# Where the rows of the transposed x begin inside a tile, in the feed-forward blocks of an encoder layer

## The chip, the cores and the metric

The kernel runs on one core of one Trainium2 chip. The metric is the device time of one execution in microseconds (us), given as the median of several runs. Beside the runs there is one profiled execution, whose trace lists every instruction with its start and its duration; it has its own time, which differs a little from the median.

Engine names are those of the profile: PE is the matrix engine (TensorE), PEld is the part of it that loads the stationary operand of a matmul, DVE is VectorE, ACT is ScalarE, POOL is GpSimd, SP issues most of the DMAs.

## The reference

One encoder layer on x of 512 rows by 1024 columns, all in float32. It has three residual blocks, each between two RMS norms:

```python
h = swiglu(rmsnorm(x, norm_ffn1_pre), w_ffn1_in, w_ffn1_out)      # feed-forward 1
x = x + 0.5 * rmsnorm(h, norm_ffn1_post)
h = mixer(rmsnorm(x, norm_mix_pre), w_mix_in, ..., w_mix_out)      # conv and mLSTM
x = x + rmsnorm(h, norm_mix_post)
h = swiglu(rmsnorm(x, norm_ffn2_pre), w_ffn2_in, w_ffn2_out)      # feed-forward 2
x = x + 0.5 * rmsnorm(h, norm_ffn2_post)

def swiglu(x, w_in, w_out):                # w_in 1024 x 5632, w_out 2816 x 1024
    gate, up = split(x @ w_in, 2)
    return (silu(gate) * up) @ w_out
```

The change touches the operand x of `x @ w_in` in the two feed-forward blocks. The mixer takes its x from tiles that another branch of the same function makes, and these stay as they are.

## The kernel before, in words

**Numbers in two parts.** A float32 number is held as a high part (rounded to the matrix engine's fp32r) and a low part (what is left), made by `split`: ACT writes the high part, DVE subtracts. A product is the sum of three matmuls: high by high, high by low, low by high.

**Feed-forward, first half.** The hidden width 2816 is 22 column blocks of 128. Each has a gate block and an up block of `w_in`. The first two (`PLAIN = 2`) are computed plainly by `plain` (L545): for one half of the 512 rows of x, 24 matmuls (3 parts by 8 chunks of the contraction) of 256 columns. The other 20 take gate and up together in a scheme with seven products instead of eight: `w_pair` makes sums and differences of the weight blocks on DVE and splits them, and `mm_part` (L519) runs each product as 12 matmuls (3 parts by 4 chunks) of 256 columns. So one column block is 84 matmuls at L519, one block of the network 20 times 84 = 1680 of them and 8 times 24 = 192 at L545; both feed-forward blocks together have 3744.

**Operands of these matmuls.** The weights are stationary: 128 columns of a `whi`, `wlo` or `ws` tile, loaded anew for each matmul. The transposed x is the moving operand: 256 columns. It lies in eight tiles per block, made by `xq_tile` and cut by `xq_hl`: four for the quarters of x (half of the width by half of the rows) and four, `t1` to `t4`, for the combinations that the seven products need (`combine_x`). Each tile has four rows `q`, one for each chunk of the contraction. In a row the first 256 numbers are the high part and the next 256 the low part. A matmul reads 256 numbers of one row, 1024 bytes in each partition, and consecutive matmuls of a product go through the rows q = 0, 1, 2, 3.

**Where the rows lie.** All tiles of the pool `big` are made by `wide` with 4 times 528 = 2112 numbers, 8448 bytes, in each partition (L64). In the built program the pool's first tile starts at byte 24256 of a partition, and the others follow every 8448 bytes. 8448 is 33 times 256, so all tiles start 192 bytes behind a multiple of 256. Most users take the first 2048 numbers as four rows of 512 (`bigt`, L67): rows 2048 bytes apart, which all start at the same place within 256 bytes. The x tiles of the feed-forward are cut by L407 into four rows of 528 instead: 2112 bytes apart, so that each starts 64 bytes further within 256 than the one before. The weight tiles all start 192 bytes behind a multiple of 256, and so do their blocks of 128 numbers (512 bytes).

**Other matmuls that matter here.** In the mixer, `seven` calls the same `mm_part` with x tiles of the `"m"` branch, made by `bigt`: there all rows start at the same place. L726 is the second half of the feed-forward (`product_out`), with 512 columns of weights as the moving operand; its operands too start at that one place. L953 is the mixer's v projection: x is stationary there, and the moving operand is a weight tile of four rows of 528 (`v_split`), in pairs of matmuls of 256 and of 272 columns.

**What sets the order.** A scheduler places the instructions of each engine; `pin` holds some of them in the order of the program. Weights are fetched by SP through `w_load` and split one block ahead by `w_split`.

Of the kernel before, what the change touches and what calls it, by code (L numbers as in the profile page):

```python
# [8 lines left out]
F32 = mybir.dt.float32  # L9
F32R = mybir.dt.float32r  # L10
# [26 lines left out]
BW = 528  # L37
# [4 lines left out]
def encoder_kernel(ctx: ExitStack, tc: tile.TileContext, a: dict, out: bass.AP):  # L42
# [16 lines left out]
    def nm(s):  # L59
        uid[0] += 1  # L60
        return f"{s}_{uid[0]}"

    def wide(dt=F32):
        return big.tile([P, 4 * BW], dt, tag="big", name=nm("big"))  # L64

    def bigt(dt=F32):
        return wide(dt)[:, 0:2048].rearrange("p (q f) -> p q f", q=4)  # L67

    def ps():
        return psum.tile([P, 512], F32, tag="ps", name=nm("ps"))  # L70
# [333 lines left out]

    def xq_tile(xq, key):
        if key not in xq["q"]:
            xq["q"][key] = bigt(F32R) if "m" in xq else wide(F32R).rearrange("p (q f) -> p q f", q=4)  # L407
        return xq["q"][key]

    def xq_hl(xq, key):  # L410
        if "m" in xq and isinstance(key, tuple):
            return tuple(xq_tile(xq, (key[0], v))[:, :, blk(key[1], 256)] for v in "hl")
        t = xq_tile(xq, key)
        return t[:, :, 0:256], t[:, :, 256:512]

    def flip_q(tb, xs, xq, halves=(0, 1), bank=None):

        full = []
        for b in halves:
            pt = bank or ps()  # L420
            for k in range(4):
                pin(nc.tensor.transpose(out=pt[:, blk(k)], in_=xs[:, blk(4 * b + k)], identity=ident))  # L422
            hi, lo = xq_hl(xq, (b, tb // 2))
            split(hi[:, :, blk(tb % 2)], lo[:, :, blk(tb % 2)], ch(pt))
            if b not in xq["f"]:
                xq["f"][b] = bigt()
            if bank:
                return lambda fn: pin(fn(xq["f"][b][:, :, blk(tb)], ch(pt)))
            full.append((b, pt))
        for b, pt in full:  # L430
            pin(nc.scalar.copy(xq["f"][b][:, :, blk(tb)], ch(pt)))
# [74 lines left out]
    def mm_cols(o, w, xq):  # L506
        n = 0
        for ww, xx in ((0, "h"), (0, "l"), (1, "h")):
            for k in range(KD):
                nc.tensor.matmul(  # L510
                    o, w[ww][:, k, :], xq_tile(xq, (k // 4, xx))[:, k % 4, FULL], start=n == 0, stop=n == 3 * KD - 1)
                n += 1
# [10 lines left out]
    def ffn(xq, between, finish, mid=None, within=None, ahead=(2, 2, 1, 1), late=None, prep=None, block=0):  # L523
# [4 lines left out]


        h = [bigt() for _ in range((NF + 3) // 4)]  # L530
        spare.extend(h[-1][:, q, 0:512] for q in (2, 3))

# [399 lines left out]
    xq = st["xq"]  # L932
# [2 lines left out]
        return xq_hl(xq, (k // 4, tb // 2))[hl][:, k % 4, blk(tb % 2)]  # L935


    vaug = wide().rearrange("p (q f) -> p q f", q=4)
    vv = vaug.rearrange("p c (h e) -> p c h e", e=BW // 4)
    nc.gpsimd.memset(vv[:, :, :, DV:DV + 1], 1.0)  # L940
    spread = t2()
# [308 lines left out]
        pn2[:, 256:272], parl, acd.rearrange("p q c -> p (q c)"),  # L1250
        start=True, stop=True,
    )
    Ct = wide().rearrange("p (q f) -> p q f", q=4)
    Cf = Ct.rearrange("p q f -> p (q f)")
    Cs = Cf[:, 0:12 * 129].rearrange("p (q i e) -> p q i e", q=4, i=3)
    nat1 = Cf[:, 1552:2064].rearrange("p (c r) -> p c r", r=P)
# [215 lines left out]
```

## Time and profile before

| what | value |
|---|---|
| median of 3 runs | 885.02 us (884.16 to 885.32) |
| the profiled execution's own time | 884.01 us |
| its span in the trace | 882.1 us |
| mean granted TensorE clock | 0.998 |
| PE busy | 873.4 us, 99% of the span |
| DVE busy | 731.5 us, 83% |
| ACT busy | 492.9 us, 56% |

The span runs from the first instruction to the last of the profiled execution; 1.9 us of its time lie around it. Durations in the groups are those of single instructions. Matmuls overlap each other, so the duration of one (280 ns in the feed-forward) is more than the distance from one start to the next; that distance is had from the chain of waits, which lists stretches of the chain with their length and their count of instructions.

### The profile page before, as it was taken

The page shows a single profiled execution, that of the slowest core. Times are in us where ns is not written, and L with a number is a line of the kernel's source. Part 1 is how long each engine was busy: PE and PEld are TensorE (multiplying, and loading weights), DVE is VectorE, ACT ScalarE, POOL GpSimd, SP SyncE. Part 2 cuts the span into 40 slices and gives each one's busy share as a digit, 9 for nine tenths or more (in the row PEclk, how much of TensorE's full clock was granted, in tenths as well). Part 3 has the DMA queues.
Part 4 walks back from the last instruction along what each step waited for, and adds up shares of the span by engine and source line. Part 5 has one row for each costly group of instructions (what it writes and reads, how often), then busy time and mean ns, then how long its engine had stood idle before and what let it go on. Part 6 is the DMA issues. An engine that isn't in the chain of part 4 may idle for free.

```text
span 882.1 us, 15403 instructions
## 1 busy us (share of the span) xinstructions
PE 873.4 (99%) x6039; PEld 808.1 (92%) x6039; DVE 731.5 (83%) x1159; ACT 492.9 (56%) x855; POOL 93.6 (11%) x123
## 2 busy tenths in 40 slices
PE   8999999999999999999999999999999999999997
PEld 7999999999988889988998988999999999988885
DVE  7989898988889978887588757897898888869956
ACT  7655556544657645755475536555555555546722
POOL 5000000001232023100121011000000000223000
PEclk9999999999999999999999999999999999999999
DMA  9444333435998852442063733433333423899722
GB/s 263 121 121 134 106 95 98 120 88 130 227 246 200 279 180 86 121 119 72 1 191 96 223 112 106 130 100 97 96 96 98 138 77 109 202 243 229 268 74 95
DMA packets 140384, 123.24 MB, mean 140 GB/s; under 512 B 5500, under 2 KB 116112, under 8 KB 140312
## 3 DMA queue, kind: packets, MB, share of 16 engines
q1 hardware_dynamic: 129936, 97.62, 37.0%
q0 software_dynamic: 10368, 24.65, 12.6%
q8 instruction: 47, 0.77, 0.4%
q14 instruction: 25, 0.20, 0.1%
q10 hardware_dynamic: 8, 0.01, 0.0%
HBM read 115.96 MB, written 6.29 MB: 139 GB/s over the span
## 4 chain that ended last, share of the span: by engine, by line
PE 98%; DVE 0%; ACT 0%; issue 0%; POOL 0%; DVEq 0%; POOLq 0%; ACTq 0%
PE ps L519 48%; PE ps L726 19%; PE ps L510 9%; PE ps L545 5%; PE ps L1428 5%; PE ps L748 5%; PE ps L953 3%; PE ps L1331 1%; PE ps L422 1%; PE ps L1339 0%; PE ps L475 0%; PE ps L1280 0%; PE ps L1307 0%; PE ps L1300 0%; PE ps L1373 0%
## 5 line engine op out<-in xcount | busy, mean ns | idle before, releaser
L519 PE MATMUL ps<-big,whi 128*128 128x256 f32 x2064 | 284.1, 281 | 0.0
L519 PEld LDWEIGHTS ps<-big,whi 128*128 128x128 f32 x2064 | 261.4, 188 | 1.1 <-ACT t L1312 0.2
L366 ACT CAST whi<-raw 128x1024 fp32r<-128x1024 f32 x170 | 175.6, 1051 | 68.5 <-DVE raw L219 23.7
L369 DVE TENSOR_TENSOR wlo<-raw,whi 128x1024 fp32r<-128x1024 f32 x166 | 201.1, 1218 | 12.1 <-ACT whi L366 7.8
L519 PE MATMUL ps<-big,wlo 128*128 128x256 f32 x1032 | 161.8, 280 | 0.0
L519 PEld LDWEIGHTS ps<-big,wlo 128*128 128x128 f32 x1032 | 139.0, 189 | 0.0
L726 PE MATMUL ps<-whi,big 128*128 128x512 f32 x336 | 105.7, 389 | 0.0
L726 PEld LDWEIGHTS ps<-whi,big 128*128 128x128 f32 x336 | 62.9, 188 | 13.0
L519 PE MATMUL ps<-big,ws 128*128 128x256 f32 x516 | 70.0, 280 | 0.0
L173 POOL DMA_DIRECT2D raw<-in_w_ffn_out_dram x18 | 22.2, 1232 | 442.3 <-DMA raw<-in_w_ffn_out_dram 226.3
L519 PEld LDWEIGHTS ps<-big,ws 128*128 128x128 f32 x516 | 64.8, 188 | 0.0
L726 PE MATMUL ps<-wlo,big 128*128 128x512 f32 x168 | 64.8, 389 | 0.0
L693 ACT COPY t<-ps 128x256 f32<-128x256 f32 x40 | 14.9, 373 | 88.4 <-PE ps L519 88.4
L510 PE MATMUL ps<-big,whi 128*128 128x512 f32 x224 | 54.5, 394 | 0.0
L366 ACT CAST whi<-t 128x1024 fp32r<-128x1024 f32 (+1 forms) x44 | 39.5, 914 | 17.7 <-DVE t L219 10.2
L510 PEld LDWEIGHTS ps<-big,whi 128*128 128x128 f32 x224 | 41.4, 188 | 8.7
L369 DVE TENSOR_TENSOR wlo<-t,whi 128x1024 fp32r<-128x1024 f32 (+1 forms) x44 | 46.1, 1048 | 1.4 <-ACT whi L366 0.7
L748 PE MATMUL ps<-whi,big 128*128 128x512 f32 x128 | 39.8, 390 | 0.0
L726 PEld LDWEIGHTS ps<-wlo,big 128*128 128x128 f32 x168 | 31.5, 188 | 6.5
L695 DVE TENSOR_TENSOR t<-ps,t 128x256 f32<-128x256 f32 x40 | 16.9, 422 | 21.0 <-PE ps L519 20.9
L545 PE MATMUL ps<-big,whi 128*128 128x256 f32 x256 | 33.6, 282 | 0.0
L698 ACT ACTIVATE t<-t 128x512 f32<-128x512 f32 x40 | 25.2, 631 | 12.4 <-DVE t L695 12.0
(245 smaller groups left out, 1412.3 us busy)
## 6 DMA issues: line engine op xcount, KB each, us to landing
raw<-in_w_ffn_in_dram SPq DMA_DIRECT2D x68, 512.0 KB, 4.8
raw<-in_w_ffn_out_dram SPq DMA_DIRECT2D x26, 512.0 KB, 4.2
raw<-in_w_mix_in_dram SPq DMA_DIRECT2D x24, 512.0 KB, 4.2
t<-in_w_ffn_in_dram SPq DMA_DIRECT2D x20, 512.0 KB, 3.8
raw<-in_w_ffn_out_dram SPq DMA_DIRECT2D x36, 256.0 KB, 5.0
raw<-in_w_ffn_out_dram POOLq DMA_DIRECT2D x18, 512.0 KB, 7.8
xd<-x POOLq DMA_DIRECT2D x8, 512.0 KB, 2.9
x<-xd POOLq DMA_DIRECT2D x8, 512.0 KB, 5.2
```

Of the source, the lines that this page charges most:

```text
L173: nc.gpsimd.dma_start(sums.rearrange("p (g f) -> p g f", g=2), top[:, 512:1024].rearrange("p (g f) -> p g f", g=1).broadcast_to([P, 2, 512 ...
L366: latest["hi"] = nc.scalar.copy(out=hi, in_=src)
L369: latest["lo"] = eng.tensor_tensor(out=lo, in0=src, in1=f32(hi), op=ALU.subtract)
L510: nc.tensor.matmul(o, w[ww][:, k, :], xq_tile(xq, (k // 4, xx))[:, k % 4, FULL], start=n == 0, stop=n == 3 * KD - 1)
L519: pin(nc.tensor.matmul(o, ww[:, k, :], x[xx][:, k, :], start=first and n == 0, stop=n == 11, skip_group_check=True))
L545: pin(nc.tensor.matmul(o, ww[:, k, :], xq_hl(xq, (k // 4, th))[xx][:, k % 4, :], start=n == 0, stop=n == 3 * KD - 1))
L695: nc.vector.tensor_tensor(out=c[:, h1], in0=y[:, h0], in1=a_[:, h1], op=ALU.add)
L698: mark["act"] = nc.scalar.activation(c, c, AF.Silu)
L726: nc.tensor.matmul(acc[tb + t][half], left[n][x][:, blk(t)], right[n][y], start=first and x == y == 0, stop=last_ and x == 1, skip_group_c ...
L748: nc.tensor.matmul(acc[tb][half], hT[hh][:, blk(tb)], w[ww][:, blk(half, 512)], start=fresh and hh == ww == 0, stop=k == NF - 1 and hh == ...
L953: nc.tensor.matmul(pv_[i][:, 0:at.stop - at.start], xv(xx, k, tb), ww[:, k % 2, at], start=n == 0, stop=n == 3 * KD - 1)
L1428: nc.tensor.matmul(acc[half], yy[yi][:, k % 4, blk(tb)], wmo[k][wi][:, blk(half, 512)], start=(n == 0 and yi == 0 and wi == 0), stop=(n == ...
```

## The change

The x tiles of the feed-forward get rows of 512 numbers, 2048 bytes apart, and the first row begins 48 numbers (192 bytes) behind the tile's start. 48 + 4 times 512 is 2096 of the tile's 2112 numbers. All four rows of all eight tiles then start 192 + 192 = 384 bytes behind a multiple of 256, which is 128 bytes behind the next one. The tiles themselves, their number and their places stay. The two other edits write `wide` with a rearrangement as `bigt(row=BW)`, which is the same tile with the same rows.

The instructions of all five engines, their order and the semaphores that they wait for are the same in both built programs; the programs differ in the addresses with which the x tiles are written and read.

```diff
-    def bigt(dt=F32):
-        return wide(dt)[:, 0:2048].rearrange("p (q f) -> p q f", q=4)
+    def bigt(dt=F32, at=0, row=512):
+        return wide(dt)[:, at:at + 4 * row].rearrange("p (q f) -> p q f", q=4)
...
     def xq_tile(xq, key):
         if key not in xq["q"]:
-            xq["q"][key] = bigt(F32R) if "m" in xq else wide(F32R).rearrange("p (q f) -> p q f", q=4)
+            xq["q"][key] = bigt(F32R) if "m" in xq else bigt(F32R, at=48)
         return xq["q"][key]
...
-    vaug = wide().rearrange("p (q f) -> p q f", q=4)
+    vaug = bigt(row=BW)
...
-    Ct = wide().rearrange("p (q f) -> p q f", q=4)
+    Ct = bigt(row=BW)
```

## The prediction

> **What bounds the kernel now.** I read the page first, for what the end hangs on.
>
> ```profile
> span 882.1 us, 15403 instructions
> PE 98%; DVE 0%; ACT 0%; issue 0%; POOL 0%; DVEq 0%; POOLq 0%; ACTq 0%
> PE ps L519 48%; PE ps L726 19%; PE ps L510 9%; PE ps L545 5%; PE ps L1428 5%; PE ps L748 5%; PE ps L953 3%; PE ps L1331 1%; PE ps L422 1%; PE ps L1339 0%; PE ps L475 0%; PE ps L1280 0%; PE ps L1307 0%; PE ps L1300 0%; PE ps L1373 0%
> ```
>
> The chain that ended last is the matrix engine for 98% of the span, and L519 alone, the products of the feed-forward's first half, is 48% of it. So what counts is the distance from one matmul to the next. It is not in the groups, whose durations overlap, but in the chain of waits, where a piece has a start, a length and a count. These pieces have no gap in them:
>
> ```profile
> 22.68 13.25 PE ps L545 x112
> 35.93 196.41 PE ps L519 x1668
> 236.51 83.00 PE ps L726 x366
> 343.07 8.76 PE ps L953 x72
> ...
> 560.79 11.28 PE ps L545 x96
> 572.07 193.44 PE ps L519 x1644
> ```
>
> And a piece of the same L519 in the mixer, from the chain of a window there:
>
> ```profile
> 484.99 8.64 PE ps L519 x72
> ```
>
> Length by count gives the step. In the feed-forward it is 196.41 / 1668 = 117.75 ns and 193.44 / 1644 = 117.66 ns, so 117.7. In the mixer the same helper, with the same shapes, steps by 8.64 / 72 = 120.0 ns. What differs there is how the x tile is cut: the mixer's rows all start at one place within 256 bytes (192 bytes behind a multiple), the feed-forward's start at 192, 0, 64 and 128 in turn. So the placement of the moving operand has a price, and the trace shows two of its values.
>
> The groups of weight loads in windows of the two stages (first 40 to 220 us, then 485 to 493.6 us) say where it sits:
>
> ```profile
> L519 PEld LDWEIGHTS ps<-big,whi 128*128 128x128 f32 x878 | 110.7, 188 | 0.0
> ...
> L519 PEld LDWEIGHTS ps<-big,whi 128*128 128x128 f32 x39 | 5.0, 192 | 0.0
> ```
>
> The load of the next weights, which runs beside the matmul, takes 188 ns on average in the feed-forward and 192 ns in the mixer. Load and matmul seem to get in each other's way when both read at the same place within 256 bytes (the weights always start at 192), and the next matmul starts later.
>
> **The fixed part of a step.** L726 moves 512 columns and has both operands at the place 192: 83.00 / 366 = 226.8 ns. Against the mixer's 120.0 ns for 256 columns, 256 more columns cost 106.8 ns. So a step is 106.8 ns for each 256 columns and a fixed part:
>
> - both operands at 192, 256 columns: 120.0 - 106.8 = 13.2 ns; by this split the same for 512 columns;
> - the feed-forward, rows in turn at 192, 0, 64, 128: 117.7 - 106.8 = 10.9 ns;
> - L953, pairs of 256 and 272 columns, 264 on average: 8.76 us / 72 = 121.7 ns, less 106.8 * 264 / 256 = 110.1, leaves 11.5 or 11.6; I use 11.5. Its moving rows are also 2112 bytes apart, but in other shares: of 12 matmuls four read at 192, four at 0, two at 64, two at 128.
>
> **The change part by part.**
>
> *The refactored lines* (`vaug`, `Ct`) are the same tiles with the same rows: nothing. No instruction, wait, semaphore or DMA is added, removed or moved; no queue is passed.
>
> *The writes into the x tiles* are 128 numbers per row in `flip_q` and 256 in `combine_x`, on ACT and DVE. Their count and shape stay; I cost them at nothing, and bound that: DVE has room, as the window of the first block shows, so that a slowdown of some of these few writes would be covered.
>
> ```profile
> 36.00:232.00 196.00, 196.00 (x1667) 196.00 (x1666) 172.50 (x273) 103.43 (x169) 5.01 (x4) 1.00 0.42 117
> ```
>
> The columns are the window, its length, then PE, PEld, DVE, ACT, POOL busy. DVE works 172.5 of 196 us. The matmuls here could become 10% faster before DVE's work alone filled the stage, so DVE doesn't eat a gain of one or two per cent.
>
> *The reads* are the whole term. 2 blocks times (20 times 84 + 8 times 24) = 3744 matmuls read the moved rows, and all are in pieces like those above, on the path. One ns of the step is 3.74 us of the whole. After the change all their rows start at 128, with the weights still at 192. No stage of this trace has that all the time, so the fixed part at 128 has to be bounded.
>
> First reading: each place has its own price, and the feed-forward's 10.9 is their mean. Then 0, 64 and 128 together have 4 * 10.9 - 13.2 = 30.4, 10.1 each: a step of 116.9, 0.8 ns less, 3.0 us.
>
> Second reading, with L953 for a second equation: 12 * 11.5 = 138 = 4 * 13.2 + 4 p(0) + 2 (p(64) + p(128)). With the sum 30.4 this gives p(0) = 12.2, and 9.1 for each of 64 and 128: a step of 115.9, 1.8 ns less, 6.7 us.
>
> Between these two I take 1.07 ns, 4.0 us, nearer the first, since in the second an error of 0.1 ns in 11.5 moves p(128) by 0.3.
>
> Bounds beyond: the durations of single matmuls in the first block (least, median, greatest) are
>
> ```profile
> L519 PE MATMUL ps<-big,ws x240: 276/280/284, 37.2 to 225.0; 128*128 128x256 f32 x120
> L519 PE MATMUL ps<-big,ws x12: 283/283/283, 486.3 to 487.6; 128*128 128x256 f32 x12
> ```
>
> 280 goes with a step of 117.7 and the mixer's 283 (second row) with 120.0. If every one took the least, 276, the step would be about 4 ns less, 15 us in all: 870 us. That is the far end below. Above, nothing in the trace is worse for 256 columns at a fixed place than the mixer's 120.0: 2.3 ns more, 2.3 * 3.744 = 8.6 us. A gain can't be excluded by a row, a loss neither.
>
> Sum: 884.0 - 4.0 = 880.0 us for an execution like the profiled one (span 882.1 and 1.9 around it). The median of the runs shown is 1.0 us above the profiled time, so I forecast 885.0 - 4.0 = 881.0 us.
>
> [...]
>
> **The rivals.**
>
> *The price is for repeating, not for the place.* What the mixer has in common with the changed kernel is that each row starts at the same place as the row before. If stepping on by 64 bytes from matmul to matmul is what breaks up a regular meeting of load and matmul, the changed kernel falls into the mixer's rhythm: 120.0 ns, 885.0 + 8.6 = 893.6 us, slower by 1%. For it: the mixer's duration is 283/283/283 in the row above, a locked rhythm, while the feed-forward spreads from 276 to 284; and L726, with everything at one place, has the same 13.2. Against it: both rows that show the 13.2 have the matmul and the load at the *same* place, and the change makes it 128 beside 192; and L953, where each place comes at least twice running, has 11.5 and not 13.2. It decides from a fixed part above 10.9 at place 128.
>
> *Nothing happens.* [...] The mixer's 120.0 could come from something else in that stage (its neighbours on the engine, other traffic), and the placement be indifferent: 885.0 us. For it: only 72 matmuls in one piece carry the 120.0. Against it: weight loads at L519 are the same shape in both stages and DVE, ACT and DMA are no busier there, as the window of that piece shows (DVE 6.84 of 8.6 us, 80%; the first block above has 88%):
>
> ```profile
> 485.00:493.60 8.60, 8.60 (x74) 8.60 (x74) 6.84 (x15) 6.56 (x16) 1.32 (x1) 1.00 0.40 125
> ```
>
> *A place with no meeting at all.* If 64 bytes behind the load is far enough that the two never collide, the step goes to the 276 ns rows: about 870 us. For it: single durations of 276 occur. Against it: a fixed part of 10.9 - 4 = 6.9 ns is below both readings above.
>
> *The change doesn't do what it says.* All x reads come from `xq_hl`, so the new rows reach every one of the 3744; I give this no chance of its own.
>
> **How the numbers follow.** The forecast (gain of 2 to 7 us, a fixed part of 9 to 10.4) has 0.48; a gain beyond that, towards 870, 0.10; nothing, within 0.2% (1.8 us, about what a measurement of this kernel can tell from no change), 0.14; the repeat price, in full or in part, 0.28. So faster 0.58, same 0.14, slower 0.28. The likeliest case's own range is 878 to 883. For 8 in 10 it must reach to the repeat price, 893.6, and down to the second reading's 6.7 us with a little more: 877.5. What is left out is most of the 0.10 below.
>
> **What would show it right or wrong.** In the changed kernel's chain the long L519 pieces should be about 1650 matmuls in 116.6 ns each, 193 us in place of 196.4 (count alike); the weight loads of L519 in 40 to 220 us should have a mean of 187 or 188 with no tail to 193; the mixer's 120.0 and L726's 226.8 should stay. If the repeat price rules, L519 shows 120.0 ns and loads of 192 in the feed-forward too. If nothing happens, 117.7 stays. I am wrong in the working if the total moves and the L519 step doesn't: then the path would run through DVE or ACT in these stages, and the waits of PE there would no longer be empty.

## The result, and the profile after

| | before | changed |
|---|---|---|
| median | 885.17 us (884.16 to 886.24, 4 executions) | 869.81 us (868.84 to 870.57, 4 executions) |
| ratio to before | | 0.9825, 95% interval 0.9813 to 0.9837 |
| the profiled execution | 884.01 us, span 882.1 | 868.84 us, span 867.0 |

The kernel became faster by 1.75%, 15.4 us, where I had forecast 4 us. The time lies outside my range, at the far end that I had priced as a rival. These four executions lie at 869 to 871 us; other executions of the same program, below, took up to 878. Two executions of kernels tried below, of 1661.35 and 887.31 us, count as slow and enter no median and no ratio.

The pieces of the chain of waits of the changed kernel (start, length, what, count) that answer to those of before:

```profile
22.97 12.87 PE ps L545 x112
35.84 189.04 PE ps L519 x1668
229.03 82.96 PE ps L726 x366
...
477.46 8.64 PE ps L519 x72
...
553.22 10.88 PE ps L545 x96
564.10 186.32 PE ps L519 x1644
```

The two long L519 pieces have the counts of before and are 7.37 and 7.12 us shorter: 14.5 of the 15.1 us between the spans. The step is 189.04 / 1668 = 113.33 ns in both blocks, against 117.7. The mixer's 72 matmuls still step by 120.0 ns (8.64 / 72), and L726's 512 columns by 82.96 / 366 = 226.7.

The instructions of L519 in the first block of the changed kernel (least, median, greatest duration in ns, first and last start):

```profile
L519 PE MATMUL ps<-big,whi x951: 276/276/276, 35.8 to 224.1; 128*128 128x256 f32 x191
L519 PEld LDWEIGHTS ps<-big,whi x949: 187/188/188, 35.9 to 224.0; 128*128 128x128 f32 x190
```

Before, the same rows were

```profile
L519 PE MATMUL ps<-big,whi x952: 276/280/290, 35.8 to 231.6; 128*128 128x256 f32 x191
L519 PEld LDWEIGHTS ps<-big,whi x950: 187/188/193, 35.9 to 231.5; 128*128 128x128 f32 x190
```

Every matmul of this row now takes what was the least duration before: 276 ns, 951 times without one exception. The tail of the weight loads to 193 ns is gone too, but their median was 188 and is 188.

### The profile page after: what moved, and what is told of

Its sections match the earlier page's. It is cut to its first block, busy times and chain, and to the rows that moved or that the text cites. A ratio compares the mean times of both kernels' runs of the same rounds, so it can differ in the third digit from the quotient of the medians.

```text
span 867.0 us, 15403 instructions
## 1 busy us (share of the span) xinstructions
PE 858.2 (99%) x6039; PEld 792.8 (91%) x6039; DVE 730.7 (84%) x1159; ACT 491.5 (57%) x855; POOL 94.6 (11%) x123
## 4 chain that ended last, share of the span: by engine, by line
PE 98%; DVE 0%; DMA 0%; issue 0%; POOL 0%; DVEq 0%; POOLq 0%; ACT 0%; ACTq 0%
PE ps L519 47%; PE ps L726 20%; PE ps L510 9%; PE ps L545 5%; PE ps L1428 5%; PE ps L748 5%; PE ps L953 3%; PE ps L1331 1%; PE ps L422 1%; PE ps L1339 0%; PE ps L475 0%; DMA g_row<-in_norm_ffn_pre_dram 0%; PE ps L1280 0%; PE ps L1307 0%; PE ps L1300 0%; PE ps L1373 0%
## 5 line engine op out<-in xcount | busy, mean ns | idle before, releaser
L519 PE MATMUL ps<-big,whi 128*128 128x256 f32 x2064 | 275.9, 277 | 0.0
L519 PEld LDWEIGHTS ps<-big,whi 128*128 128x128 f32 x2064 | 254.1, 188 | 1.1 <-ACT t L1312 0.2
L519 PE MATMUL ps<-big,wlo 128*128 128x256 f32 x1032 | 157.7, 277 | 0.0
L519 PEld LDWEIGHTS ps<-big,wlo 128*128 128x128 f32 x1032 | 135.9, 188 | 0.0
L726 PE MATMUL ps<-whi,big 128*128 128x512 f32 x336 | 105.6, 389 | 0.0
L726 PEld LDWEIGHTS ps<-whi,big 128*128 128x128 f32 x336 | 62.9, 188 | 12.8
L519 PE MATMUL ps<-big,ws 128*128 128x256 f32 x516 | 68.0, 276 | 0.0
L726 PE MATMUL ps<-wlo,big 128*128 128x512 f32 x168 | 64.7, 389 | 0.0
L519 PEld LDWEIGHTS ps<-big,ws 128*128 128x128 f32 x516 | 62.9, 188 | 0.0
L510 PE MATMUL ps<-big,whi 128*128 128x512 f32 x224 | 54.5, 394 | 0.0
L510 PEld LDWEIGHTS ps<-big,whi 128*128 128x128 f32 x224 | 41.4, 188 | 8.7
L366 ACT CAST whi<-t 128x1024 fp32r<-128x1024 f32 (+1 forms) x44 | 39.5, 914 | 15.1 <-DVE t L219 11.3
L748 PE MATMUL ps<-whi,big 128*128 128x512 f32 x128 | 39.8, 390 | 0.0
L726 PEld LDWEIGHTS ps<-wlo,big 128*128 128x128 f32 x168 | 31.5, 188 | 6.4
L545 PE MATMUL ps<-big,whi 128*128 128x256 f32 x256 | 33.2, 280 | 0.0
L698 ACT ACTIVATE t<-t 128x512 f32<-128x512 f32 x40 | 25.2, 629 | 12.2 <-DVE t L695 12.0
L545 PEld LDWEIGHTS ps<-big,whi 128*128 128x128 f32 x256 | 31.1, 188 | 0.6 <-ACT big L366 0.3
```

The source lines that it names most:

```text
L366: latest["hi"] = nc.scalar.copy(out=hi, in_=src)
L510: nc.tensor.matmul(o, w[ww][:, k, :], xq_tile(xq, (k // 4, xx))[:, k % 4, FULL], start=n == 0, stop=n == 3 * KD - 1)
L519: pin(nc.tensor.matmul(o, ww[:, k, :], x[xx][:, k, :], start=first and n == 0, stop=n == 11, skip_group_check=True))
L545: pin(nc.tensor.matmul(o, ww[:, k, :], xq_hl(xq, (k // 4, th))[xx][:, k % 4, :], start=n == 0, stop=n == 3 * KD - 1))
L698: mark["act"] = nc.scalar.activation(c, c, AF.Silu)
L726: nc.tensor.matmul(acc[tb + t][half], left[n][x][:, blk(t)], right[n][y], start=first and x == y == 0, stop=last_ and x == 1, skip_group_c ...
```

## The experiments

The theories that the expectations number: **1**, the step follows the distance between the place of the moving rows and the place of the weights, both within 256 bytes; **2**, any one place for all rows locks into a short rhythm; **3**, only the place of the moving rows against 128 bytes counts; **4**, only the place of the moving rows counts. Distance here is place of the moving row less place of the weights, so the changed kernel has -64 bytes. Unless told otherwise an edit is made to the changed kernel.

### All rows at another place

```diff
-            xq["q"][key] = bigt(F32R) if "m" in xq else bigt(F32R, at=48)
+            xq["q"][key] = bigt(F32R) if "m" in xq else bigt(F32R, at=0)
```

> Edit: the feed-forward's x rows stay 2048 bytes apart, but begin at the tile's start, so that all lie at place 192 within 256 bytes, where the weights are too (as the mixer's x does). Theory 1 (the step follows the distance between the place of the moving rows and the place of the weights, here 0): the L519 and L545 steps go to the mixer's 120.0 ns, weight loads to 192 ns, the total to about 885.2 + 3744 * 2.3 ns = 893.8 us. Theory 2 (any one place for all rows locks into a short rhythm, and the mixer's 120.0 has another cause): 113.3 ns as in the changed kernel, about 870 us. Theory 3 (only the place of the moving rows against 128 bytes matters, and the weights do not): 120.0 ns, 893.8 us.

With `at=16`:

> Edit: the feed-forward's x rows 2048 bytes apart, begin 64 bytes further in the tile: all at place 0 within 256 bytes, 64 bytes behind the weights' 192. Theory 1 (distance to the weights): a price of its own for the distance +64; from the two readings of the prediction between 10.1 and 12.2 ns of fixed part, a step of 117 to 119 ns, total 882 to 890 us. Theory 2 (any one place): 113.3 ns, 870 us. Theory 3 (a multiple of 128 bytes is quick): 113.3 ns, 870 us.

With `at=32`:

> Edit: the feed-forward's x rows 2048 bytes apart, begin 128 bytes further in the tile: all at place 64, half of 256 bytes away from the weights' 192. Theory 1 (distance to the weights): the distance is the greatest, the step lies between 113.3 and 117.7 ns, total 869 to 885 us. Theory 2 (any one place): 113.3 ns, 870 us. Theory 3 (not a multiple of 128 bytes): 120.0 ns, 893.8 us.

| place (distance) | step of block 1, block 2 | median | ratio to before |
|---|---|---|---|
| 192 (0) | 120.0, 120.0 ns | 893.40 us | 1.0092 (1.0072 to 1.0112) |
| 0 (+64) | 117.8, 117.8 | 885.32 | 1.0004 (0.9995 to 1.0014) |
| 64 (128) | 120.0, 118.7 | 889.78 | 1.0055 (1.0040 to 1.0070) |
| 128 (-64), the change | 113.3, 113.3 | 869.81 | 0.9825 (0.9813 to 0.9837) |

The steps are the long L519 pieces by their counts; place 192 has

```profile
37.01 200.16 PE ps L519 x1668
577.89 197.28 PE ps L519 x1644
```

and its weight loads and matmuls are those of the mixer, 192 and 283 ns:

```profile
L519 PEld LDWEIGHTS ps<-big,whi x907: 191/192/193, 39.6 to 229.9; 128*128 128x128 f32 x182
L519 PE MATMUL ps<-big,whi x906: 282/283/284, 39.7 to 229.9; 128*128 128x256 f32 x182
```

Theory 2 falls: one place for all rows is not enough. Theory 3 falls too, since place 0 is a multiple of 128 and gives 117.8. Under theory 1 I had expected a step below 117.7 ns at place 64, where the distance is greatest. That was missed: the price does not simply fall with the distance. Putting all rows at the tile's start, without the 192 bytes, costs 9 us in place of gaining 15.

### The same distance by other means

Everything 64 bytes further in memory:

```diff
-    const = ctx.enter_context(tc.tile_pool(name="const", bufs=1))
+    const = ctx.enter_context(tc.tile_pool(name="const", bufs=1)); const.tile([P, 16], F32, name="pad")
```

> Edit: the changed kernel with 64 bytes of unused memory in each partition ahead of all large pools, so that every tile lies 64 bytes further: weights at place 0 and the feed-forward's x rows at place 192, still 64 bytes behind the weights in the circle of 256. Theory 1 (the distance between the two counts): 113.3 ns a step as in the changed kernel, with 117.8 where the other rhythm is picked; total 869 to 885 us. Theory 3 (the place of the moving rows against 128 bytes counts, and the weights do not): place 192 is no multiple of 128, 120.0 ns, 893.5 us.

Measured: 869.79 us median, four executions of 868.66 to 869.97 and one of 876.76, the profiled one; ratio 0.9818 (0.9802 to 0.9835). Its chain:

```profile
36.31 196.45 PE ps L519 x1668
485.47 8.64 PE ps L519 x72
572.12 186.32 PE ps L519 x1644
```

The mixer, now at place 0 with weights at place 0, still steps by 120.0 ns; the feed-forward, at place 192 with weights at 0, by 113.3 in one block and 117.8 in the other. Place 192 alone had given 120.0.

The weights, and all pools made behind them, 64 bytes further, the x rows at place 192:

```diff
-    big = ctx.enter_context(tc.tile_pool(name="big", bufs=13))
+    big = ctx.enter_context(tc.tile_pool(name="big", bufs=13)); ctx.enter_context(tc.tile_pool(name="padp", bufs=1)).tile([P, 16], F32, tag="pad", name="pad")
...
-            xq["q"][key] = bigt(F32R) if "m" in xq else bigt(F32R, at=48)
+            xq["q"][key] = bigt(F32R) if "m" in xq else bigt(F32R)
```

> Edit: the feed-forward's x rows at the tile's start (place 192, which gave 120.0 ns and 893.5 us), and 64 unused bytes ahead of the weight tiles and all pools behind them, so that the weights move to place 0 while the x tiles stay. Theory 1 (only the distance from the weights to the moving rows counts): the distance is -64 again, so the L519 step in the feed-forward is 113.3 or 117.8 ns, and in the mixer too, in place of 120.0. Theory 4 (the place of the moving rows alone counts, whatever the weights do): 120.0 ns. Other matmuls change with it: L510 (512 columns) gets distance -64, where moving the mixer's x gave 233.3 ns in place of 226.8; L726, L748 and L1428 move weights at place 0 against stationary tiles at 192, a distance of +64, which no run shows for 512 columns: between 220 and 233 ns, each ns 1.14 us in all.

Measured: 872.89 us (872.33 to 873.40), ratio 0.9862 (0.9847 to 0.9877).

```profile
36.26 189.04 PE ps L519 x1668
368.90 27.53 PE ps L510 x118
480.90 8.17 PE ps L519 x72
567.75 186.32 PE ps L519 x1644
763.72 79.65 PE ps L726 x348
```

The x rows lie where they gave 120.0 ns; with the weights moved they give 113.3, and the mixer's piece falls from 8.64 to 8.17 us (113.5 ns). So theory 4 falls and theory 1 holds: what counts is the distance between the two operands. Distance -64 ran with the places 128 and 192 and with 192 and 0, distance 0 with both operands at 192 and with both at 0, and each gave the same steps. The other pools always moved along with the weights; that it is the weights and not these is argued, from a step that stays the same through 1668 matmuls while the other engines come and go. Most of the 3 us that this kernel is behind the change comes from the 512-column matmuls: L510 at distance -64 takes 27.53 / 118 = 233.3 ns, L726 at +64 takes 79.65 / 348 = 228.9, where L510 had 26.78 / 118 = 226.9 and L726 226.7 at distance 0.

### 512 columns

```diff
-            xq["q"][key] = bigt(F32R) if "m" in xq else bigt(F32R, at=48)
+            xq["q"][key] = bigt(F32R, at=48)
```

> Edit: the changed kernel, and the mixer's x tiles also begin 192 bytes further (place 128). It reaches 252 matmuls of 256 columns at L519, 336 of 512 columns at L510 (moving) and 192 at L953 (stationary). Theories 1 and 3: L519 in the mixer goes from 120.0 to 113.3 ns (1.7 us in all); if the fixed part is the same for 512 columns, L510 goes from 226.8 to about 220.1 ns (2.2 us); total about 866 us. Theory 2 (the mixer's 120.0 has another cause): the mixer's steps stay, total 870 us.

Measured: executions of 877.27, 868.99, 870.97 and 876.37 us, ratio 0.9871 (0.9829 to 0.9914). In the profiled one (877.27):

```profile
35.80 196.45 PE ps L519 x1668
374.85 27.53 PE ps L510 x118
486.50 8.17 PE ps L519 x72
572.39 186.32 PE ps L519 x1644
```

The mixer's 256-column matmuls gain (113.5 ns), its 512-column ones lose as much as I had hoped they would gain: 233.3 ns. So the distance that is quick for 256 columns, 113.5 against 120.0 ns at distance 0, is slow for 512, 233.3 against 226.9. The expected 866 us was missed with it. And the first block, which this edit does not touch, ran at 117.8 ns: here the two rhythms showed for the first time.

The stationary tiles of the second half at another place:

```diff
-                t = bigt(F32R).rearrange("p q f -> p (q f)")
+                t = bigt(F32R, at=32).rearrange("p q f -> p (q f)")
...
-                bigt(F32R).rearrange("p q f -> p (q f)")[:, 0:2048].rearrange("p (g f) -> p g f", g=2) for _ in range(2))
+                bigt(F32R, at=32).rearrange("p q f -> p (q f)")[:, 0:2048].rearrange("p (g f) -> p g f", g=2) for _ in range(2))
...
-                    hs = bigt(F32R)
+                    hs = bigt(F32R, at=32)
```

> Edit: the changed kernel, and the stationary tiles of the feed-forward's second half that lie in the large pool begin 128 bytes further (place 64, the moving weights stay at 192): for L748 and most of L726 the moving rows are 128 bytes from the stationary ones, for those of L726 that read the tiles named xl the distance stays 0. If the fixed part of 512 columns follows the distance as that of 256 columns does (13.2 ns at distance 0, 11.9 to 13.2 at 128), L726 stays within 1.3 ns of 226.8. If 512 columns have another law (233.3 at -64 speaks for it), it can go either way, down to about 220 or up to 233 ns: 780 matmuls, 5 us either way. The first half stays in one of its two rhythms.

Measured: 881.13 us (873.33 to 881.89), ratio 0.9933 (0.9902 to 0.9963). In the profiled execution both first halves had the quick rhythm, and the second halves were slower:

```profile
36.43 189.04 PE ps L519 x1668
229.66 84.65 PE ps L726 x366
843.50 22.32 PE ps L748 x96
```

L726 steps by 231.3 ns with nearly a quarter of it unmoved, L748 by 22.32 / 96 = 232.5. So for 512 columns 0 is the best of the four distances that ran: 226.7 at 0, 228.9 at +64, 233.3 at -64, 232.5 at 128.

### How narrow the good distance is

`at=56`, `at=40`, and later `at=52`, `at=44`, `at=50`, `at=46`:

> Edit: the feed-forward's x rows 2048 bytes apart, begin 224 bytes further in the tile: all at place 160, 32 bytes from the weights' 192 and no multiple of 64. If the price follows the distance smoothly, the step lies between 113.3 (distance -64) and 120.0 ns (distance 0): about 117 ns, 882 us. If reads go in pieces of 64 bytes, a start in the middle of one adds a piece to every read: more than at either neighbour, 120 ns or above, 893 us or more.

> Edit: the feed-forward's x rows 2048 bytes apart, begin 160 bytes further in the tile: all at place 96, 96 bytes behind the weights' 192 and no multiple of 64. If the price follows the distance smoothly, the step lies between 113.3 (distance -64) and 119.3 ns (distance -128): about 116 ns, 879 us. If reads go in pieces of 64 bytes, 120 ns or above, 893 us or more.

> Edit: the feed-forward's x rows begin at place 144, 48 bytes before the weights' 192 in place of 64. If the quick rhythm needs a start at a multiple of 64 bytes: no 113.3, a step between the 118.3 of distance -32 and 117.8: 884 to 887 us. If it needs a window of distances around -64: 113.3 ns in one or both blocks, 870 to 877 us.

> Edit: the feed-forward's x rows begin at place 112, 80 bytes before the weights' 192. If the quick rhythm needs a start at a multiple of 64 bytes: a step between 117.3 and 118.7 ns as at distance -96, 884 to 888 us. If it needs a window of distances around -64: 113.3 ns in one or both blocks, 870 to 877 us.

> Edit: the feed-forward's x rows begin at place 136, 56 bytes before the weights' 192, no multiple of 16. Multiple-of-64 reading: no quick rhythm, 884 us or more. Window reading: 113.3 ns in one or both blocks, 870 to 877 us. If pieces of 16 bytes count, worse than 48 and 64 bytes.

> Edit: the feed-forward's x rows begin at place 120, 72 bytes before the weights' 192, no multiple of 16. Multiple-of-64 reading: no quick rhythm, 884 us or more. Window reading: 113.3 ns in one or both blocks, 870 to 877 us. If pieces of 16 bytes count, worse than 64 and 80 bytes.

| distance | step of block 1, block 2 | median | ratio to before |
|---|---|---|---|
| -32 | 118.3, 118.3 ns | 887.36 us | 1.0024 (1.0015 to 1.0034) |
| -48 | 119.2, 119.2 | 890.41 | 1.0054 (1.0039 to 1.0069) |
| -56 | 120.0, 121.7 | 896.04 | 1.0120 (1.0103 to 1.0137) |
| -64 | 113.3 or 117.8 | 869 to 878 | 0.982 to 0.991 |
| -72 | 120.0, 120.0 | 894.57 | 1.0101 (1.0086 to 1.0116) |
| -80 | 119.3, 119.3 | 890.49 | 1.0058 (1.0043 to 1.0073) |
| -96 | 117.3, 118.7 | 888.02 | 1.0028 (1.0017 to 1.0039) |

It is a single point and no valley: 8 bytes to either side costs as much as distance 0, or more. The row of the chain for -56 against the 186.32 of the change:

```profile
577.38 200.02 PE ps L519 x1644
```

Of the starts that are no multiples of 64 bytes, those at 32 bytes from one (-32 and -96: 117.3 to 118.7 ns) are better than those at 16 (-48 and -80: 119.2 and 119.3), and those at 16 better than those at 8 (-56 and -72: 120.0 to 121.7). The smooth reading falls: it had put 117 ns at -32 and 116 at -96. A quick step came at a multiple of 64 only, but the sizes expected by that reading were missed too: 120 ns or more at -32 and -96, where 117.3 to 118.7 came, and at most 118.7 at -48 and -80, where 119.2 and 119.3 came. Nor is a multiple of 64 enough alone: 0, +64 and 128 are multiples of 64 as well.

### Two rhythms at one distance

The changed kernel again, unedited, on two other chips:

> No edit: the changed kernel once more, on the chip of the following runs and with more executions. The run with the mixer's x moved showed the first block (which that edit does not touch) at 117.8 ns a step and the second at 113.3, and its times fell into two groups, 869 to 871 and 876 to 877 us. Theory A (the distance of 64 bytes allows two rhythms, and chance at the start of a block picks one): the times fall into groups about 7.4 us apart (1668 times 4.45 ns): 869, 877 and perhaps 884 us. Theory B (the two rhythms came with that edit): all between 868 and 871 us.

> No edit: the changed kernel on the chip of the run beside it. Times in the groups 869 to 871 and 876 to 878 us, by the rhythm of the first block, which the profile shows as 189.0 or 196.5 us for the 1668 products.

Measured: 876.46, 877.05, 877.49, 876.62 us on the one (ratio 0.9905, 0.9890 to 0.9919), and 877.63, 872.99, 870.93, 869.14 on the other (0.9863, 0.9825 to 0.9901); 872.99 lies between the expected groups. The long pieces of the profiled execution of the one (876.46 us) and then of the other (877.63 us):

```profile
35.96 196.45 PE ps L519 x1668
571.64 186.32 PE ps L519 x1644
```

```profile
37.04 196.45 PE ps L519 x1668
572.76 186.32 PE ps L519 x1644
```

196.45 - 189.04 = 7.4 us is the distance between the groups. So the same program runs its first block at 113.3 or at 117.8 ns a step, and keeps the rhythm through all 1668. The slow step of 117.8 ns is also the one of distance +64, where ten executions of 884.27 to 885.78 us showed no quick one. Places 64, 96 and 136 have two steps in one execution as well (the tables above). The L545 matmuls of the first repeat, before and after 25.9 us, show where it changed there:

```profile
L545 PE MATMUL ps<-big,whi x17: 276/276/277, 22.9 to 25.7; 128*128 128x256 f32 x17
...
L545 PE MATMUL ps<-big,whi x52: 281/281/286, 25.9 to 34.7; 128*128 128x256 f32 x52
```

276 goes with the step of 113.3, 281 with 117.8, about 163 ns less in both cases; by that the longest, of 286, is a step of about 123 ns, a matmul that came late by 5 ns against 117.8 and 10 against 113.3. This step is my estimate from the durations. The list of waits of PE from 10 to 40 us has one wait, of 0.5 us at L422, and none so short. In the profile of the other repeat (877.63 us) the L545 piece behind the transposes, from 23.77 us on, takes 13.27 us for 112 matmuls, 118.5 ns each, where this one takes 13.09 and the quick execution (868.84 us) 12.87: no quick stretch shows in its length. Two runs tried to fix the rhythm. First, four transposes ahead of the loop:

```diff
-            a_, u, c = t2(), t2(), t2()
+            a_, u, c = t2(), t2(), t2(); [pin(nc.tensor.transpose(out=x[:, blk(i)], in_=ident, identity=ident)) for i in range(4 * (j == PLAIN))]
```

> Edit: the changed kernel, and ahead of the first product of the seven-product loop the matrix engine transposes the identity four times into the PSUM tile that the product then overwrites (about 0.6 us in each block; it computes nothing that is used). In the profiled runs so far stretches at the distance -64 that began right behind transposes went to 113.3 ns nearly always, those behind a wait or behind 512-column matmuls mostly to 117.8. If the way in picks the rhythm, both blocks go at 113.3 ns in nearly every execution: 869 to 871 us, no group at 877. If chance picks it whatever comes before, the times fall into the groups 870 and 877 as before.

Measured: 877.97 us (877.27 to 878.72), ratio 0.9919 (0.9905 to 0.9934). In the profiled execution the first block ran at 113.3 and the second at 117.8:

```profile
37.09 189.06 PE ps L519 x1668
566.32 193.86 PE ps L519 x1646
```

A miss: with transposes ahead of both blocks, one had the quick rhythm and the other had not. (The scheduler also placed other matmuls in another order.) Second, the wait that I supposed behind the late step taken away, by splitting the next weights behind the last x:

```diff
-(3, 0): lambda: mark.update(latest), (3, 1): lambda: flip_q(3, st1[3], xT1),
+(3, 1): lambda: (flip_q(3, st1[3], xT1), mark.update(latest)),
```

> Edit: in the first block the split of the next pair of weights is placed behind the splits of the fourth row block's x instead of ahead of them, so that DVE has that x's low part ready some 3 us earlier and no matmul waits for it; the scheduler places some later matmuls in another order. If a disturbed step picks the rhythm: from the transposes before it (113.3 ns behind them in the four profiles that I looked at) the first block stays at 113.3 ns to its end, all executions at 868 to 871 us unless the second block is slow. If chance picks it at each start: groups at 870 and 877 us in the first block as before. A new wait, later and elsewhere, would show as another change of rhythm at that place.

Measured: 876.75 us (876.69 to 877.19), ratio 0.9909 (0.9893 to 0.9926). The L545 of the first block ahead of the last transposes and behind them:

```profile
L545 PE MATMUL ps<-big,whi x22: 276/276/276, 14.9 to 18.2; 128*128 128x256 f32 x22
...
L545 PE MATMUL ps<-big,whi x72: 281/281/364, 23.0 to 35.2; 128*128 128x256 f32 x72
```

The piece from 23.26 us on takes 13.19 us for 112 matmuls, 117.8 ns each, so no late step shows in its length, and the rhythm held; but it was the one of 117.8 ns, there from the transposes on, where I had expected 113.3. I had also expected that a later wait would show as another change of rhythm. A wait came at 49.2 us and changed nothing; the step is 117.9 ns ahead of it and behind it:

```profile
36.46 12.73 PE ps L519 x108
...
50.64 181.17 PE ps L519 x1536
```

The quick execution of the changed kernel (868.84 us) has late steps too: near 25.9 us its L545 shows a matmul of 289 ns and one of 383 ns, and from 26.3 us on all have 276 again. So a rhythm lasted for a whole block here (1668 matmuls in 189.04 or in 196.45 us), and a late step came with a change of rhythm in one profile and left it as it was in another. What picks it, neither run could set. That stays open, and so does whether a kernel can be had at 870 us in each execution. No version that ran beats the change.

## Why the prediction was wrong, point by point

- **What bounds the kernel, and what the change touches: right.** The chain is PE for 98%, and 14.5 of 15.1 us came from the two long L519 pieces; L726, the mixer's L519 and L953 did not move.
- **The reading that placement has a price, and that the weights are the other side of it: right, and now shown.** The distance decides; the mixer's 120.0 ns is the price of distance 0, and the kernel with x at place 192 in the feed-forward has it too, at 893.40 us, where "the price is for repeating" had put 893.6. That rival named the right step for the wrong reason: it is the distance 0, and not the repeating, since the changed kernel repeats its place too.
- **The step that failed, a mis-sized term: p(128).** I took 9.8 ns, where 6.5 came. I shared what 10.9 leaves for the other three places evenly (10.1 each), or by a second equation from L953 (9.1 for 64 and for 128). By the steps at one fixed place, less 106.8 ns, p(192) is 13.2, p(0) 11.0, p(64) 11.9 to 13.2, and p(128) 6.5 in the quick rhythm or 11.0 in the other. With 6.5 their mean is 10.7 to 11.0, about the 10.9 of the mixed rows, so the first reading's sum was right and its even split wrong. The second reading's split was wrong in each term that it gave (12.2 for 0, 9.1 for 64). 3.74 us for each ns, times 4.4 in place of 1.07, is 16.5 us in place of 4.0; 15.4 came, in part since some stretches of L545 ran at 117.7 (10.36 us for 88).
- **The split of a step into 106.8 ns for each 256 columns and a fixed part: not general.** At distance 0 the two widths differ by 226.7 - 120.0 = 106.7 ns, but at -64 by 233.3 - 113.3 = 120.0. The first reading needs only differences between 256-column steps and does not hang on this; the second one, with L953's 264 columns, does.
- **Where I chose: the argument against the far end was circular.** I rejected 870 us because its 6.9 ns lay below both readings, and the readings were assumptions on how to split a sum. The row itself, with 276 among the durations, was better evidence, since it showed that single matmuls had it. The range should have reached 870. That rival's time came, but its reason, that 64 bytes are far enough apart, is not what the runs show: at 64 bytes to the other side, and at 72, 80, 96 and 128 bytes apart, the step is 117.3 to 120.0 ns.
- **The sign of a good step: half right.** Loads of 187 and 188 ns with no tail were forecast and came, but the median load was 188 before as well, while the step fell by 4.4 ns. Nor does the load's median tell the two rhythms apart: in the first block it is 188 ns at the step of 113.3 (868.84 us) and at that of 117.8 (876.46 us), with a greatest of 188 and of 192; at distance 0, with 120.0, it is 192.
- **One number for one distance: wrong.** No part of the prediction allowed the same program two steady steps. In other executions of the same program the first block runs at 117.8, and the gain is 8 us and not 15.
- **A misread line against "nothing happens".** I wrote that ACT is no busier in the mixer's window; it is, 6.56 of 8.6 us (76%) beside 103.43 of 196 (53%). The kernel with x at place 192 answers the rival without that line: it has the mixer's 120.0 ns in the feed-forward.
- **DVE has room: right.** In the first block of the changed kernel it is busy 171.8 of 188 us, and PE had no gap there:

```profile
36.00:224.00 188.00, 188.00 (x1661) 188.00 (x1660) 171.79 (x274) 102.78 (x169) 4.88 (x4) 1.00 0.44 122
```

- **That load and matmul get in each other's way: my guess, and not shown.** The kernel took 870 us with the rows at place 128 and 893 at place 192, by an edit of the place alone. No run here shows what the matmuls wait for, only that the relative place of the operands costs up to 8 ns of 120 in each matmul (113.3 to 121.7 ns).

## What to carry to other kernels

When the chain is one engine that issues the same instruction thousands of times, divide the length of a long piece by its count and compare stages that differ in layout: a step of 120.0 beside one of 117.7 ns, with the same shapes, can be a price of the layout, to be tested by moving one operand alone. A few bytes of offset were worth 8 to 15 us here. The good offset was one point between bad neighbours, so try offsets against the other operand one by one, multiples of 64 bytes first, instead of reasoning out a trend, and try them for each width apart. When rows that mix several places give only a mean, don't share it evenly among them: let the range reach to the best duration that occurs. Look at several executions of the same program before a gain of one per cent is put down to an edit, since this one has two rhythms that are 0.8% apart.

## What the runs showed of the hardware that I had not expected

- The step of fp32r matmuls with a new weight load each depends on the distance between moving and stationary operand: 113.3 to 121.7 ns for 256 columns, 226.7 to 233.3 for 512. At -64 bytes 256 columns are quicker than at 0, and 512 columns slower.
- Four of the steady steps are multiples of one small time: 113.33, 120.0, 226.67 and 233.3 ns are 17, 18, 34 and 35 times 6.67 ns, which is what 16 columns (64 bytes) take at 106.7 ns for 256. Others, such as 118.3 and 119.2, are not, and no run shows what the small time is.
- A rhythm of the matrix engine lasted 196.45 us unchanged in one profile, 1668 matmuls with 281 ns in every record. In that profile the L545 stretch in which it had set in, from 25.9 us on, has a longest matmul of 286 ns; in others longer ones (289 and 383 ns near 25.9 us in the quick execution), or a wait at 49.2 us, changed nothing.
